# A gated DeltaNet stage on one core: convolution taps that read PSUM, an inverse that goes block by block, and small scalings on other engines

## The chip, the cores and the metric

The kernel runs on one core of a Trainium2 chip (trn2). The metric is the device time of one execution in microseconds. In the profile TensorE is PE (its weight loads PEld), VectorE is DVE, ScalarE is ACT, GpSimd is POOL, and SyncE, which issues the loads of the weights, is SP.

## The reference

Two transformer blocks run over one sequence of 256 tokens and 1024 features. The change touches one branch of the second block, a DeltaNet of 8 heads of 128 features, once forward and once backward over the sequence:

```python
def gated_deltanet_branch(qkv, z, b_in, a_in, conv_w, a_log, dt_bias, o_gain):
    qkv = jax.nn.silu(centred_depthwise_conv(qkv, conv_w))     # 5 taps, zeros at both ends
    q, k, v = jnp.split(qkv, 3, axis=-1)
    q, k, v = l2_norm(heads(q)), l2_norm(heads(k)), heads(v)
    ...
    o_fwd = chunk_gated_delta_rule(q, k, v, g[0], beta[0])
    o_bwd = flip(chunk_gated_delta_rule(flip(q), flip(k), flip(v), flip(g[1]), flip(beta[1])))
    o = rms_norm_2(o, o_gain) * jax.nn.silu(zf)

def chunk_gated_delta_rule(q, k, v, g, beta):
    ...
    lower = jnp.where(strict, jnp.einsum('bhnik,bhnjk->bhnij', k_beta, kc) * decay, 0.0)
    t_inv = lax.linalg.triangular_solve(eye + lower, eye, left_side=True, lower=True, unit_diagonal=True)
    u = t_inv @ v_beta
    w = t_inv @ (k_beta * jnp.exp(gc)[..., None])
    ...
```

The reference takes chunks of 64 tokens; the kernel computes the same function with chunks of 128, so that each head has two chunks and each chunk needs the inverse of a triangular 128x128 matrix.

## The kernel before

**Stages.** The first block runs up to about 833 us of the span and is the same in both kernels. The second block has a front stage (`block2_front`, line 1457), which computes the DeltaNet and the projections of an attention with compressed keys; then that attention, an output projection, and 16 experts, whose weights (201 MB) stream through `in_w_ex` loads of 2 MB. Those loads need the memory of the front stage's pools, so the first of them is issued when that stage ends.

**Blocks and groups.** The projection `w_qkv` has 24 blocks: q, k and v of 8 heads. A block is 24 TensorE matmuls into one PSUM bank: 8 pieces of the contracted features, each in three products of rounded parts and remainders (`mm3`, lines 169 to 171). The rounded part of a piece of weights is made by ScalarE (line 144), the remainder by VectorE (line 146). `head_in` (line 936) takes a finished block `ps`. It copies it on ScalarE into a tile `cz` with two zero columns at each end, which GpSimd sets (lines 943 to 945), scales it by the middle tap on ScalarE (line 947), and adds the four other taps on VectorE (line 949), each one 128x256 operation that reads `cz` and `cv` and writes `cv`. Then come a tanh (line 977) and the silu's product (line 978), two transposes on TensorE into another bank `pt` (line 958), and norms. The projection's `ps` and the transposes' `pt` come from the same pool of PSUM banks, tag "A", which has two.

**The chain of a group.** Two heads are a group; its chain is the generator `group` (line 1008): decays (line 1001), the matrices X (lines 1032 to 1037), and for 8 matrices at once (two directions, two chunks, two heads) the inverse Z of I + X with its transpose W (in the trace: X is AT, W is Y, Z is YT). Blocks of 16 on the diagonal are inverted column by column on VectorE (lines 1061, 1062). Then three levels join blocks of 16, 32 and 64:

```python
for m in range(8): matmul(ps[:, m], x[:, m], wv[:, m])      # line 1079, 128x128 by 64 columns
n1 = ps * mask of the level                                 # line 1081, VectorE, 128x512
for m in range(8): matmul(p2[:, m], z[:, m], n1[:, m])      # line 1094
wv = wv - p2                                                # line 1095, VectorE
8 transposes of W into PSUM, 2 copies into Z                # lines 1100, 1101 (ScalarE)
```

Level 64 needs no transposes: its second products go to half of the columns of Z or of W (lines 1087, 1089) and VectorE subtracts them (lines 1090, 1091). After the levels come the states and outputs of the two chunks (lines 1110 to 1162), with small per-token factors in a tile `small` (lines 1111 to 1116), a sum of squares `qs` (line 1024), and products with columns (`vs` line 1129, `vn1` line 1130, `q1` line 1149), all on VectorE.

**Order.** `block2_front` runs six slots. In a slot the steps of one group's projection, of the first part of the chain of the group before and of the rest of the chain of the one before that are traced in turns (`zip_longest`, line 1540). The framework then gives each engine one fixed order of instructions, made from the trace's priorities and its own planning of when operands and banks are ready. An engine whose next instruction must wait holds all that stand behind it.

Of the kernel before, what the change touches and what calls it, by code (L numbers as in the profile page):

```python
# [86 lines left out]
class B:  # L87
    """Shared helpers: streams of weight pieces, projections, norms."""
# [14 lines left out]
    def phase(self, ctx, banks, psum=None):  # L103
        """pools of one part of the kernel; banks: PSUM banks per tag; psum: what those close with, if not ctx."""
# [27 lines left out]
    def stream(self, name, group=1, pool=0):  # L132
        """Pieces of a weight, in order, each as (rounded part, remainder); pool: GpSimd subtracts one in so many."""
# [15 lines left out]
    def staged(self, n, first, second, fills):  # L149
        """second(i, first(i)) for each i, one first ahead; fills: spare blocks at the start, then per i."""  # L150
# [1599 lines left out]
```

## Time and profile before

| what | value |
|---|---|
| runs | 1752.5, 1753.26, 1753.8 us; median 1753.26 |
| profiled execution, span | 1749.7 us |
| around the span, to the median | 3.6 us |
| PE busy over the span | 1531.4 us (88%) |
| DVE busy | 919.8 us (53%) |
| ACT busy | 659.8 us (38%) |
| POOL busy | 115.5 us (7%) |

The profiled execution is shown by its span alone, from its first to its last instruction; what the device time has beside it is the third row. The busy shares are averages over stages with different limits. A row of the windows' view gives, for a stretch of the span, each engine's busy time, the TensorE clock that was granted as a share of full speed, and the share of time in which the DMA engines moved data. A row by shape gives the busy time of a group of instructions, the mean duration of one in ns, and the idle time of the engine just before them with what ended it. In a timeline an instruction's start is given in us from the span's start; matmuls overlap, so that their pace is the distance of their starts.

### The profile page before, as it was taken

How to read it: one execution, taken by the hardware profiler on the slowest of the kernel's cores; microseconds unless marked ns; L12 is line 12 of the kernel's file. 1: busy time of each engine (PE TensorE's matmuls, PEld its weight loads, DVE VectorE, ACT ScalarE, POOL GpSimd, SP SyncE). 2: the span in 40 equal slices, each digit the busy share in tenths (PEclk: the TensorE clock that was granted, in tenths of full speed). 3: DMA queues.
4: the chain of work that ended last, by engine and by line, in shares of the span. 5: the costliest groups of instructions: out<-in, count | busy, mean ns of one | idle time of the engine just before them, and what ended most of it. 6: DMA issues, size and time to landing. Idle time of an engine off the chain costs nothing. (4 is left out here: it accounts for less than half of the span.)

```text
span 1749.7 us, 25276 instructions
## 1 busy us (share of the span) xinstructions
PE 1531.4 (88%) x9987; PEld 1192.8 (68%) x9987; DVE 919.8 (53%) x1685; ACT 659.8 (38%) x1181; POOL 115.5 (7%) x196
## 2 busy tenths in 40 slices
PE   7999999999999999999879999999989856656565
PEld 7989889998887888999768878867764301211112
DVE  7665677656566567755898986545651200101001
ACT  7444554445554544444754433455321100000000
POOL 0000000000000000000251431100000000000000
PEclk9999999999999999999889999999989988878878
DMA  6655489655545348865413122356769999999997
GB/s 238 184 182 164 148 282 315 219 186 175 167 136 168 121 168 300 294 193 178 138 49 98 60 85 85 134 194 246 267 233 372 427 428 427 427 428 426 428 428 313
DMA packets 76887, 416.08 MB, mean 238 GB/s; under 512 B 9696, under 2 KB 10976, under 8 KB 64480
## 3 DMA queue, kind: packets, MB, share of 16 engines
q1 hardware_dynamic: 76768, 414.47, 64.4%
q8 instruction: 78, 1.28, 0.3%
q14 instruction: 41, 0.34, 0.1%
HBM read 413.38 MB, written 1.05 MB: 237 GB/s over the span
## 5 line engine op out<-in xcount | busy, mean ns | idle before, releaser
L146 DVE TENSOR_TENSOR wl<-st,wh 128x1024 fp32r<-128x1024 f32 x350 | 429.0, 1228 | 241.2 <-PE ps L171 99.1
L144 ACT CAST wh<-st 128x1024 fp32r<-128x1024 f32 x350 | 366.6, 1049 | 426.4 <-PE ps L170 124.9
L171 PE MATMUL ps<-ah,wl 128*128 128x256 f32 x1152 | 324.0, 282 | 5.1 <-DVE wl L146 4.8
L169 PE MATMUL ps<-ah,wh 128*128 128x256 f32 x1152 | 323.7, 281 | 0.2
L170 PE MATMUL ps<-al,wh 128*128 128x256 f32 x1152 | 322.5, 280 | 0.0
L171 PEld LDWEIGHTS ps<-ah,wl 128*128 128x128 f32 x1152 | 216.8, 188 | 8.5 <-DVE wl L146 8.2
L169 PEld LDWEIGHTS ps<-ah,wh 128*128 128x128 f32 x1152 | 216.8, 188 | 2.8 <-ACT wh L144 0.6
L170 PEld LDWEIGHTS ps<-al,wh 128*128 128x128 f32 x1152 | 216.2, 188 | 2.0
L1340 PE MATMUL ps<-ex,slot 128*32 128x512 f32 x512 | 86.9, 812 | 63.1 <-DMA ex<-in_w_ex 63.1
L1298 DVE TENSOR_TENSOR room<-room,ps 128x512 f32<-128x512 f32 x8 | 5.5, 687 | 221.0 <-PE ps L1340 221.0
L169 PE MATMUL ps<-wh,ah 128*128 128x512 f32 x288 | 115.3, 400 | 0.0
L170 PE MATMUL ps<-wl,ah 128*128 128x512 f32 x288 | 114.4, 397 | 0.0
L171 PE MATMUL ps<-wh,al 128*128 128x512 f32 x288 | 114.1, 397 | 0.0
L1340 PE MATMUL ps<-ex,room 128*32 128x256 f32 (+1 forms) x768 | 74.7, 536 | 37.1 <-DMA ex<-in_w_ex 36.8
L1340 PE MATMUL ps<-ex,xe 128*32 128x512 f32 x512 | 77.2, 689 | 32.8 <-DMA ex<-in_w_ex 32.6
L1297 ACT ACTIVATE room<-ps 128x512 f32<-128x512 f32 x8 | 4.7, 596 | 268.1 <-PE ps L1340 268.0
L1340 PEld LDWEIGHTS ps<-ex,slot 128*32 128x32 f32 x512 | 16.0, 130 | 131.4 <-DMA ex<-in_w_ex 101.6
L1340 PEld LDWEIGHTS ps<-ex,room 128*32 128x32 f32 x768 | 26.2, 123 | 82.8 <-DMA ex<-in_w_ex 36.6
L808 DVE SCALAR_TENSOR_TENSOR sm<-sm,csil 128x1024 f32<-128x1024 f32 x48 | 58.6, 1223 | 25.3 <-DMA sm<-in_w_mod 25.1
L169 PE MATMUL ps<-wh,yh 128*128 128x512 f32 x176 | 69.6, 395 | 0.4 <-ACT yh L183 0.4
L170 PE MATMUL ps<-wl,yh 128*128 128x512 f32 x176 | 69.5, 395 | 0.0
L171 PE MATMUL ps<-wh,yl 128*128 128x512 f32 x176 | 69.4, 394 | 0.0
(494 smaller groups left out, 2608.3 us busy)
## 6 DMA issues: line engine op xcount, KB each, us to landing
ex<-in_w_ex SPq DMA_DIRECT2D x94, 2048.0 KB, 39.1
st<-in_w_ff SPq DMA_DIRECT2D x132, 512.0 KB, 4.1
sm<-in_w_mod SPq DMA_DIRECT2D x48, 512.0 KB, 5.1
st<-in_w_ci SPq DMA_DIRECT2D x24, 512.0 KB, 3.6
st<-in_w_qkv SPq DMA_DIRECT2D x24, 512.0 KB, 3.3
st<-in_w_mk SPq DMA_DIRECT2D x16, 512.0 KB, 3.6
st<-in_w_mv SPq DMA_DIRECT2D x16, 512.0 KB, 3.5
st<-in_w_mq SPq DMA_DIRECT2D x16, 512.0 KB, 3.6
```

The source lines that it names most:

```text
L144: nc.scalar.copy(hi[:, :w], st[:, q, :w])
L146: e.tensor_tensor(lo[:, :w], st[:, q, :w], hi[:, :w].bitcast(F32), ALU.subtract)
L169: mm(ps, lh[0], rh[0], start=start, stop=False)
L170: mm(ps, lh[0], rh[1], start=False, stop=False)
L171: mm(ps, lh[1], rh[0], start=False, stop=stop)
L808: nc.vector.scalar_tensor_tensor(st, st, 1.0, self.sc, ALU.mult, ALU.mult, accum_out=m[:, k:k + 1])
L1297: nc.scalar.activation(hid[:, s], gu[0][f], AF.Silu)
L1298: nc.vector.tensor_tensor(hid[:, s], hid[:, s], gu[1][f], ALU.mult)
L1340: b.nc.tensor.matmul(ps[32 * j:32 * j + 32], lhs[:, 32 * j:32 * j + 32], w[:, j], start=k == 0, stop=k == KC - 1)
```

## The change

Three parts of the DeltaNet are written anew; all else is the same.

1. **Taps.** The tile `cz`, its two GpSimd memsets and ScalarE's copy are gone. The four taps read the PSUM bank `ps` itself, over 254 or 255 columns, so that no zeros are needed. The bank is now released by the last tap.
2. **Levels 32 and 64.** Level 16 stays. Level 32 multiplies only blocks that can be other than zero: 16 products of 32x32, two copies of 32x256 (ScalarE and VectorE), 24 products of 32x32 that give the blocks of Z and of W directly, and four multiplications by -1 (three on ScalarE, one on VectorE). The mask, 8 transposes and two copies are gone. Level 64 has 8 products of 64x64, a ScalarE copy, 8 products, and a multiplication by -1 on each of VectorE and ScalarE instead of two subtractions.
3. **Small scalings.** `small` has three rows instead of four: one memset on GpSimd and two copies on ScalarE, for two memsets and three copies on VectorE. `qs` goes to GpSimd. `vn1` becomes two ScalarE scalings of 128x128 and a copy of 128x256, `q1` four ScalarE scalings of 128x128, each in place of one VectorE product of 128x512.

```diff
-LEVELS = (16, 32, 64)
...
-    lv = []
-    for b_ in LEVELS:
-        c = r[r // b_ % 2 == 0][None, :]
-        lv.append(f((k // (2 * b_) == c // (2 * b_)) & (k // b_ % 2 == 1)))
-    a['m_lev'] = np.concatenate(lv, axis=1)
+    c = r[r // SUB % 2 == 0][None, :]
+    a['m_lev'] = f((k // (2 * SUB) == c // (2 * SUB)) & (k // SUB % 2 == 1))
...
-        self.sub, self.lev = (c('m_sub', 8 + SUB), c('m_lev', len(LEVELS) * 64))
+        self.sub, self.lev = (c('m_sub', 8 + SUB), c('m_lev', 64))
...
-        z = b.sp.tile([P, T + 4], F32, tag='cz', name=b.nm('cz'))
-        nc.gpsimd.memset(z[:, 0:2], 0.0)
-        nc.gpsimd.memset(z[:, T + 2:], 0.0)
-        nc.scalar.copy(z[:, 2:T + 2], ps)
...
-            nc.vector.scalar_tensor_tensor(v, z[:, t:t + T], w(t), v, ALU.mult, ALU.add)
+            to, of = (slice(2 - t, T), slice(0, T + t - 2)) if t < 2 else (slice(0, T + 2 - t), slice(t - 2, T))
+            nc.vector.scalar_tensor_tensor(v[:, to], ps[:, of], w(t), v[:, to], ALU.mult, ALU.add)
...
-        nc.vector.tensor_scalar(self.qs[:, :, hs], self.qs[:, :, hs], EPS * P, EPS * EPS * P, ALU.mult, ALU.add)
+        nc.gpsimd.tensor_scalar(self.qs[:, :, hs], self.qs[:, :, hs], EPS * P, EPS * EPS * P, ALU.mult, ALU.add)
...
-        for li, bs in enumerate(LEVELS):
-            yield True
-            wv = W.rearrange('p d t h (n s c) -> p (d t h) n s c', s=2, c=bs)[:, :, :, 0]
-            n1 = b.dp.tile([P, 8, 64], F32, tag='n1', name=b.nm('n1'), bufs=2)
-            ps = b.psum(tag).rearrange('p (m c) -> p m c', m=8)
-            for m in range(8):
-                nc.tensor.matmul(ps[:, m].rearrange('p (n c) -> p n c', c=bs), x[:, m], wv[:, m], start=True, stop=True)
-            nc.vector.tensor_tensor(n1, ps, mid(self.lev[:, li * 64:li * 64 + 64], 8), ALU.mult)
-            p2 = b.psum(tag).rearrange('p (m c) -> p m c', m=8)
-            if bs == 64:
-                for m in range(8):
-                    if m < 4:
-                        nc.tensor.matmul(p2[0:64, m], n1[:, m], z[:, m, 64:], start=True, stop=True)
-                    else:
-                        nc.tensor.matmul(p2[64:, m], z[:, m, 64:], n1[:, m], start=True, stop=True)
-                nc.vector.tensor_tensor(z[0:64, 0:4, 64:], z[0:64, 0:4, 64:], p2[0:64, 0:4], ALU.subtract)
-                nc.vector.tensor_tensor(w[64:, 4:8, 0:64], w[64:, 4:8, 0:64], p2[64:, 4:8], ALU.subtract)
-                break
-            for m in range(8):
-                nc.tensor.matmul(p2[:, m], z[:, m], n1[:, m], start=True, stop=True)
-            nc.vector.tensor_tensor(wv, wv, p2.rearrange('p m (n c) -> p m n c', c=bs), ALU.subtract)
-            for d in range(2):
-                s = slice(4 * d, 4 * d + 4)
-                p3 = b.psum(tag).rearrange('p (h i) -> p h i', h=4)
-                for m in range(4):
-                    nc.tensor.transpose(p3[:, m], w[:, 4 * d + m], b.eye)
-                nc.scalar.copy(z[:, s], p3)
+        yield True
+        bs = SUB
+        wv = W.rearrange('p d t h (n s c) -> p (d t h) n s c', s=2, c=bs)[:, :, :, 0]
+        n1 = b.dp.tile([P, 8, 64], F32, tag='n1', name=b.nm('n1'), bufs=2)
+        ps = b.psum(tag).rearrange('p (m c) -> p m c', m=8)
+        for m in range(8):
+            nc.tensor.matmul(ps[:, m].rearrange('p (n c) -> p n c', c=bs), x[:, m], wv[:, m], start=True, stop=True)
+        nc.vector.tensor_tensor(n1, ps, mid(self.lev, 8), ALU.mult)
+        p2 = b.psum(tag).rearrange('p (m c) -> p m c', m=8)
+        for m in range(8):
+            nc.tensor.matmul(p2[:, m], z[:, m], n1[:, m], start=True, stop=True)
+        nc.vector.tensor_tensor(wv, wv, p2.rearrange('p m (n c) -> p m n c', c=bs), ALU.subtract)
+        for d in range(2):
+            s = slice(4 * d, 4 * d + 4)
+            p3 = b.psum(tag).rearrange('p (h i) -> p h i', h=4)
+            for m in range(4):
+                nc.tensor.transpose(p3[:, m], w[:, 4 * d + m], b.eye)
+            nc.scalar.copy(z[:, s], p3)
+        yield True
+        n1 = b.dp.tile([P, 8, 64], F32, tag='n1', name=b.nm('n1'), bufs=2)[:, :, 0:32]
+        q = [slice(32 * i, 32 * i + 32) for i in range(4)]
+        ps = b.psum(tag)[:, 0:T].rearrange('p (m c) -> p m c', m=8)
+        for m in range(8):
+            for i in (0, 2):
+                nc.tensor.matmul(ps[q[i + 1], m], x[q[i], m, q[i + 1]], w[q[i], m, q[i]], start=True, stop=True)
+        nc.scalar.copy(n1[q[1]], ps[q[1]])
+        nc.vector.tensor_copy(n1[q[3]], ps[q[3]])
+        p2 = b.psum(tag)[:, 0:T].rearrange('p (m c) -> p m c', m=8)
+        for m in range(8):
+            nc.tensor.matmul(p2[q[1], m], z[q[1], m, q[1]], n1[q[1], m], start=True, stop=True)
+            nc.tensor.matmul(p2[q[2], m], n1[q[3], m], z[q[3], m, q[3]], start=True, stop=True)
+            if m < 4:
+                nc.tensor.matmul(p2[q[0], m], n1[q[1], m], z[q[1], m, q[1]], start=True, stop=True)
+            else:
+                nc.tensor.matmul(p2[q[3], m], z[q[3], m, q[3]], n1[q[3], m], start=True, stop=True)
+        nc.scalar.mul(w[q[1], :, q[0]], p2[q[1]], -1.0)
+        nc.vector.tensor_scalar(z[q[2], :, q[3]], p2[q[2]], -1.0, None, ALU.mult)
+        nc.scalar.mul(z[q[0], 0:4, q[1]], p2[q[0], 0:4], -1.0)
+        nc.scalar.mul(w[q[3], 4:8, q[2]], p2[q[3], 4:8], -1.0)
+        yield True
+        n1 = b.dp.tile([P, 8, 64], F32, tag='n1', name=b.nm('n1'), bufs=2)
+        ps = b.psum(tag).rearrange('p (m c) -> p m c', m=8)
+        for m in range(8):
+            nc.tensor.matmul(ps[64:, m], x[0:64, m, 64:], w[0:64, m, 0:64], start=True, stop=True)
+        nc.scalar.copy(n1[64:], ps[64:])
+        p2 = b.psum(tag).rearrange('p (m c) -> p m c', m=8)
+        for m in range(8):
+            if m < 4:
+                nc.tensor.matmul(p2[0:64, m], n1[64:, m], z[64:, m, 64:], start=True, stop=True)
+            else:
+                nc.tensor.matmul(p2[64:, m], z[64:, m, 64:], n1[64:, m], start=True, stop=True)
+        nc.vector.tensor_scalar(z[0:64, 0:4, 64:], p2[0:64, 0:4], -1.0, None, ALU.mult)
+        nc.scalar.mul(w[64:, 4:8, 0:64], p2[64:, 4:8], -1.0)
...
-        small = b.sp.tile([P, 4, 2, 2], F32, tag='small', name=b.nm('small'))
-        be0, be1, es, neg_eg = [small[:, i] for i in range(4)]
-        for n, be in enumerate((be0, be1)):
-            nc.vector.memset(be[:, 1], 1.0)
-            nc.vector.tensor_copy(be[:, 0], beta[:, n, 0])
+        small = b.sp.tile([P, 3, 2, 2], F32, tag='small', name=b.nm('small'))
+        be1, es, neg_eg = [small[:, i] for i in range(3)]
+        nc.gpsimd.memset(be1[:, 1], 1.0)
+        nc.scalar.copy(be1[:, 0], beta[:, 1, 0])
...
-        nc.vector.tensor_copy(es[:, 1], self.es[:, 1, hs])
+        nc.scalar.copy(es[:, 1], self.es[:, 1, hs])
...
-        nc.vector.tensor_tensor(vn1, ps, col(be0), ALU.mult)
+        for h in range(2):
+            nc.scalar.mul(vn1[:, 0, h], ps[:, 0, h], beta[:, 0, 0, h:h + 1])
+        nc.scalar.copy(vn1[:, 1], ps[:, 1])
...
-        nc.vector.tensor_tensor(q1, ps, col(self.eg[:, :, hs]), ALU.mult)
+        for d, h in dh:
+            nc.scalar.mul(q1[:, d, h], ps[:, d, h], self.eg[:, d, h0 + h:h0 + h + 1])
```

In the changed kernel the taps are line 943, the transposes of a block line 952, level 32 lines 1093 to 1108, level 64 lines 1114 to 1123.

**TensorE, in the first group's projection, before.** `ps_1487_8900` is the fourth block's bank, `ps_1464_8775` the bank of the first block's transposes.

```order
L958 MATMUL ps_1464_8775<-c_eye_67,qkT_1454_8728 128x128 x2
L169 MATMUL ps_1487_8900<-ak_1424_8523,wh_1486_8897 128x256
L170 MATMUL ps_1487_8900<-ak_1424_8523,wh_1486_8897 128x256
L171 MATMUL ps_1487_8900<-ak_1424_8523,wl_1485_8896 128x256
L169 MATMUL ps_1487_8900<-ak_1424_8523,wh_1486_8897 128x256
```

**The same place now.** `ps_1476_8839` is the third block's bank, `ps_1463_8771` that of the first block's transposes.

```order
L171 MATMUL ps_1476_8839<-ak_1424_8523,wl_1474_8835 128x256
L169 MATMUL ps_1476_8839<-ak_1424_8523,wh_1475_8836 128x256
L170 MATMUL ps_1476_8839<-ak_1424_8523,wh_1475_8836 128x256
L952 MATMUL ps_1463_8771<-c_eye_67,qkT_1454_8728 128x128 x2
L171 MATMUL ps_1476_8839<-ak_1424_8523,wl_1474_8835 128x256
L169 MATMUL ps_1476_8839<-ak_1424_8523,wh_1475_8836 128x256
L170 MATMUL ps_1476_8839<-ak_1424_8523,wh_1475_8836 128x256
```

The transposes of a block stood behind the whole projection of the block two further on; they now stand inside it, behind 8 of its 24 matmuls here and behind 14 one block later. They take the bank that held the block between the two, which the taps of that block release.

**VectorE, where level 32 of the first group meets the taps of a block, before.** `n1`, `Y` and the `ps` beside them belong to the level, `t16` and `z16` to the blocks of 16 of the next group.

```order
L1081 TENSOR_TENSOR n1_1664_9754<-ps_1665_9755,m_lev_8688 128x512
L949 SCALAR_TENSOR_TENSOR cv_1660_9739<-cz_1659_9735,cols2_2228,cv_1660_9739 128x256
L1061 TENSOR_TENSOR t16_1670_9792<-ps_1669_9787,z16_1654_9698 128x8x15
L949 SCALAR_TENSOR_TENSOR cv_1660_9739<-cz_1659_9735,cols2_2228,cv_1660_9739 128x256
L1062 TENSOR_TENSOR z16_1654_9698<-z16_1654_9698,t16_1670_9792 128x8x15
L1095 TENSOR_TENSOR Y_1513_9053<-Y_1513_9053,ps_1666_9765 128x16x32
L978 SCALAR_TENSOR_TENSOR vraw_1661_9745<-th_1662_9746,cv_1660_9739 128x256
```

**The same place now.**

```order
L943 SCALAR_TENSOR_TENSOR cv_1645_9679<-ps_1644_9654,cols2_2228,cv_1645_9679 128x254
L1055 TENSOR_TENSOR t16_1653_9748<-ps_1652_9743,z16_1640_9642 128x8x15
L943 SCALAR_TENSOR_TENSOR cv_1645_9679<-ps_1644_9654,cols2_2228,cv_1645_9679 128x255
L1056 TENSOR_TENSOR z16_1640_9642<-z16_1640_9642,t16_1653_9748 128x8x15
L943 SCALAR_TENSOR_TENSOR cv_1645_9679<-ps_1644_9654,cols2_2228,cv_1645_9679 128x255
L1106 TENSOR_SCALAR YT_1508_9030<-ps_1651_9714 32x8x32
L943 SCALAR_TENSOR_TENSOR cv_1645_9679<-ps_1644_9654,cols2_2228,cv_1645_9679 128x254
L1055 TENSOR_TENSOR t16_1654_9751<-ps_1652_9743,z16_1640_9642 128x8x14
```

Between the taps of a block stand operations of the next group's chain, as before. The level's mask and its subtraction over 128 rows are no longer there; a multiplication over 32 rows stands between the third and fourth tap, and the taps read `ps_1644_9654`.

## Rows read from the trace of the kernel before

**Rows 1.** The page, part 1: busy time and instructions.

```profile
PE 1531.4 (88%) x9987; PEld 1192.8 (68%) x9987; DVE 919.8 (53%) x1685; ACT 659.8 (38%) x1181; POOL 115.5 (7%) x196
```

**Rows 2.** Windows: us; PE, PEld, DVE, ACT, POOL; clock; DMA, GB/s.

```profile
857.00:937.00 80.00, 63.83 (x441) 58.91 (x440) 75.08 (x186) 42.38 (x112) 34.95 (x60) 0.89 0.27 88
937.00:1022.00 85.00, 78.51 (x650) 74.14 (x650) 75.19 (x192) 38.29 (x109) 25.35 (x44) 1.00 0.21 69
1022.00:1135.00 113.00, 106.02 (x711) 92.67 (x710) 73.89 (x156) 45.16 (x88) 25.42 (x29) 0.98 0.31 103
...
1312.00:1749.00 437.00, 286.30 (x2042) 90.64 (x2041) 41.09 (x93) 23.57 (x47) 3.10 (x5) 0.84 0.97 411
```

**Rows 3.** Line 1697's loads: ns min/median/max, first and last start.

```profile
L1697 SPq DMA_DIRECT2D ex<-in_w_ex x98: 327/328/1109, 1129.3 to 1704.0; - x98
```

**Rows 4.** DVE by shape, 857 to 937: busy us, mean ns, idle before.

```profile
L949 DVE SCALAR_TENSOR_TENSOR cv<-cz,cols,cv 128x256 f32<-128x256 f32 x53 | 33.2, 635 | 0.6 <-ACT cv L947 0.6
```

**Rows 5.** DVE by shape, 937 to 1022.

```profile
L949 DVE SCALAR_TENSOR_TENSOR cv<-cz,cols,cv 128x256 f32<-128x256 f32 x43 | 23.3, 543 | 1.3 <-ACT cv L947 1.2
...
L1081 DVE TENSOR_TENSOR n<-ps,m_lev 128x512 f32<-128x512 f32 x6 | 4.1, 683 | 0.5 <-PE ps L1079 0.5
...
L1130 DVE TENSOR_TENSOR vn<-ps,small 128x512 f32<-128x512 f32 x2 | 1.4, 683 | 0.0
...
L1090 DVE TENSOR_TENSOR YT<-YT,ps 64x256 f32<-64x256 f32 x2 | 0.8, 412 | 0.6 <-PE ps L1089 0.6
```

**Rows 6.** DVE by shape, 833 to 1090.

```profile
L1114 DVE COPY small<-es 128x2 f32<-128x2 f32 x4 | 3.1, 780 | 0.0
...
L1024 DVE TENSOR_SCALAR qs<-qs 128x4 f32<-128x4 f32 x4 | 2.6, 656 | 0.0
```

**Rows 7.** Line 949 alone: ns min/median/max, first and last start.

```profile
L949 DVE SCALAR_TENSOR_TENSOR cv<-cz,cols,cv x96: 466/478/1346, 859.9 to 1019.1; 128x256 f32<-128x256 f32 x96
```

**Rows 8.** Line 190 alone, the same columns.

```profile
L190 DVE SCALAR_TENSOR_TENSOR al<-ps,cols,ah x56: 473/475/485, 12.5 to 645.3; 128x256 fp32r<-128x256 f32 x56
```

**Rows 9.** GpSimd's timeline: start, duration, instruction.

```profile
910.49 2.48 POOL L1001 TENSOR_TENSOR dr<-rge,gr 128x512 fp32r<-128x512 f32 x2 [1.94 <-PE ps L1002]
```

**Rows 10.** DVE's timeline in the same stretch.

```profile
910.81 1.26 DVE L949 SCALAR_TENSOR_TENSOR cv<-cz,cols,cv 128x256 f32<-128x256 f32 x1
912.00 0.24 DVE L1061 TENSOR_TENSOR t<-ps,z 128x96 f32<-128x96 f32 x1
```

**Rows 11.** Timeline of three engines around one block.

```profile
1014.72 0.28 PE L171 MATMUL ps<-ak,wl 128*128 128x256 f32 x1
...
1016.14 0.48 ACT L947 ACTIVATE cv<-ps,cols 128x256 f32<-128x256 f32 x1
...
1016.72 0.48 DVE L949 SCALAR_TENSOR_TENSOR cv<-cz,cols,cv 128x256 f32<-128x256 f32 x1 [0.64 <-ACT cv L947]
...
1017.25 0.48 DVE L949 SCALAR_TENSOR_TENSOR cv<-cz,cols,cv 128x256 f32<-128x256 f32 x1
...
1019.09 0.48 DVE L949 SCALAR_TENSOR_TENSOR cv<-cz,cols,cv 128x256 f32<-128x256 f32 x1
```

**Rows 12.** PE by shape, 857 to 1022.

```profile
L958 PE MATMUL ps<-c_eye,qkT 128*128 128x128 f32 x32 | 6.7, 292 | 6.4 <-DVE qkT L978 5.8 <-DVE dg L876 0.4 <-DVE dg L878 0.2
```

**Rows 13.** PE's timeline, 950 to 962.

```profile
951.59 0.71 PE L1100 MATMUL ps<-c_eye,Y 128*128 128x128 f32 x5
...
953.20 1.89 PE L1079 MATMUL ps<-Y,AT 128*128 128x64 f32 x16
...
957.30 0.28 PE L171 MATMUL ps<-ak,wl 128*128 128x256 f32 x1
957.42 0.28 PE L169 MATMUL ps<-ak,wh 128*128 128x256 f32 x1
957.63 0.50 PE L1087 MATMUL ps<-YT,n 128*64 128x64 f32 x5
...
958.52 0.39 PE L170 MATMUL ps<-ak,wh 128*128 128x256 f32 x1
```

More of the change, by code (lines that the diff above doesn't have):

```diff
@@ L894, in __init__ @@
         self.le = c("m_le")
-        self.sub, self.lev = c("m_sub", 8 + SUB), c("m_lev", len(LEVELS) * 64)
+        self.sub, self.lev = c("m_sub", 8 + SUB), c("m_lev", 64)
         self.pick = b.xp.tile([P, SUB - 1, P], F32, tag="pick", name="pick")
@@ L1072, in group @@
             nc.scalar.copy(w[:, s], ps)
-        for li, bs in enumerate(LEVELS):
-            yield True
-            wv = W.rearrange("p d t h (n s c) -> p (d t h) n s c", s=2, c=bs)[:, :, :, 0]
-            n1 = b.dp.tile([P, 8, 64], F32, tag="n1", name=b.nm("n1"), bufs=2)
-            ps = b.psum(tag).rearrange("p (m c) -> p m c", m=8)
-            for m in range(8):
-                nc.tensor.matmul(ps[:, m].rearrange("p (n c) -> p n c", c=bs), x[:, m], wv[:, m],
-                                 start=True, stop=True)
-            nc.vector.tensor_tensor(n1, ps, mid(self.lev[:, li * 64:li * 64 + 64], 8), ALU.mult)
-            p2 = b.psum(tag).rearrange("p (m c) -> p m c", m=8)
-            if bs == 64:
-                for m in range(8):
-                    if m < 4:
-                        nc.tensor.matmul(p2[0:64, m], n1[:, m], z[:, m, 64:], start=True, stop=True)
-                    else:
-                        nc.tensor.matmul(p2[64:, m], z[:, m, 64:], n1[:, m], start=True, stop=True)
-                nc.vector.tensor_tensor(z[0:64, 0:4, 64:], z[0:64, 0:4, 64:], p2[0:64, 0:4], ALU.subtract)
-                nc.vector.tensor_tensor(w[64:, 4:8, 0:64], w[64:, 4:8, 0:64], p2[64:, 4:8], ALU.subtract)
-                break
-            for m in range(8):
-                nc.tensor.matmul(p2[:, m], z[:, m], n1[:, m], start=True, stop=True)
-            nc.vector.tensor_tensor(wv, wv, p2.rearrange("p m (n c) -> p m n c", c=bs), ALU.subtract)
-            for d in range(2):
-                s = slice(4 * d, 4 * d + 4)
-                p3 = b.psum(tag).rearrange("p (h i) -> p h i", h=4)
-                for m in range(4):
-                    nc.tensor.transpose(p3[:, m], w[:, 4 * d + m], b.eye)
-                nc.scalar.copy(z[:, s], p3)
@@ new lines, in group @@
+        yield True
+        bs = SUB
+        wv = W.rearrange("p d t h (n s c) -> p (d t h) n s c", s=2, c=bs)[:, :, :, 0]
+        n1 = b.dp.tile([P, 8, 64], F32, tag="n1", name=b.nm("n1"), bufs=2)
+        ps = b.psum(tag).rearrange("p (m c) -> p m c", m=8)
+        for m in range(8):
+            nc.tensor.matmul(ps[:, m].rearrange("p (n c) -> p n c", c=bs), x[:, m], wv[:, m], start=True, stop=True)
+        nc.vector.tensor_tensor(n1, ps, mid(self.lev, 8), ALU.mult)
+        p2 = b.psum(tag).rearrange("p (m c) -> p m c", m=8)
@@ new lines, in group @@
+        n1 = b.dp.tile([P, 8, 64], F32, tag="n1", name=b.nm("n1"), bufs=2)[:, :, 0:32]
+        q = [slice(32 * i, 32 * i + 32) for i in range(4)]
+        ps = b.psum(tag)[:, 0:T].rearrange("p (m c) -> p m c", m=8)
+        for m in range(8):
[3 more added lines that the diff above has]
+        nc.vector.tensor_copy(n1[q[3]], ps[q[3]])
+        p2 = b.psum(tag)[:, 0:T].rearrange("p (m c) -> p m c", m=8)
@@ L1102, in group @@
+        p2 = b.psum(tag).rearrange("p (m c) -> p m c", m=8)
+        for m in range(8):
[5 more added lines that the diff above has]
+        nc.scalar.mul(w[64:, 4:8, 0:64], p2[64:, 4:8], -1.0)
         yield True
@@ L1105, in group @@
         col = lambda a: a.rearrange("p d (h o) -> p d h o", o=1).to_broadcast([P, 2, 2, P])
-        small = b.sp.tile([P, 4, 2, 2], F32, tag="small", name=b.nm("small"))
-        be0, be1, es, neg_eg = [small[:, i] for i in range(4)]
-        for n, be in enumerate((be0, be1)):
-            nc.vector.memset(be[:, 1], 1.0)
-            nc.vector.tensor_copy(be[:, 0], beta[:, n, 0])
+        small = b.sp.tile([P, 3, 2, 2], F32, tag="small", name=b.nm("small"))
+        be1, es, neg_eg = [small[:, i] for i in range(3)]
+        nc.gpsimd.memset(be1[:, 1], 1.0)
+        nc.scalar.copy(be1[:, 0], beta[:, 1, 0])
         nc.vector.tensor_tensor(es[:, 0], self.es[:, 0, hs], beta[:, 0, 0], ALU.mult)
-        nc.vector.tensor_copy(es[:, 1], self.es[:, 1, hs])
+        nc.scalar.copy(es[:, 1], self.es[:, 1, hs])
         nc.vector.tensor_scalar(neg_eg, self.eg[:, :, hs], -1.0, None, ALU.mult)
```

10 lines of the change are left out of this document (6 added, 4 removed).

## Prediction

> **What bounds the kernel now.** I read the page's busy shares first: PE 88%, DVE 53% [rows 1]. Such shares mix stages, so I cut the span by stage [rows 2]. The last 437 us are bound by DMA (share 0.97), at 411 GB/s. Their loads begin only at 1129.3 [rows 3], when the front stage's pools are given back; so a microsecond won or lost before about 1130 moves everything behind it by as much, and one behind it is worth nothing. The changed lines run in three stretches, 857 to 937, 937 to 1022 and 1022 to 1135. In the first DVE is busy 75.08 of 80 us (94%) and PE 63.83 (80%): DVE is the bound. In the second PE has 78.51 and DVE 75.19 of 85 us: both are near it. In the third PE has 106.02 of 113 us, and DVE 65%: PE is the bound.
>
> Next I asked what DVE does in the first two. The taps come first: 53 take 33.2 us, then 43 take 23.3 us, with means of 635 and 543 ns [rows 4, 5], though half of all 96 take 478 ns or less and the longest 1346 [rows 7]. The timelines side by side show why: while GpSimd multiplies two SBUF tiles, from 910.49 on [rows 9], a tap that starts at 910.81 takes 1.26 us, and the operation behind it, whose first operand is in PSUM, takes its plain 0.24 us [rows 10]. A DVE operation with both inputs in SBUF is stretched beside GpSimd's work; one with an input in PSUM is not. Line 190, of the same operation and shape with one input in PSUM, shows the price that a changed tap should have: 473 to 485 ns over 56 instructions [rows 8].
>
> **The change part by part.**
>
> *Taps, DVE's work.* 96 taps at 475 ns are 45.6 us; now they take 33.2 + 23.3 = 56.5. DVE saves 10.9 us in 857 to 1022.
>
> The Trainium skill speaks against this: "Perfetto Trace Analysis", section "Optimizing Scalar/DVE Operations", gives a VectorE instruction some 60 ns of access overhead on SBUF and 125 ns on PSUM. An estimate by the Trainium skill is 96 x 65 ns = 6.2 us given back, and 1747 us instead of the sum below. The trace disagrees: 475 ns with PSUM against 478 without [rows 7, 8].
>
> *Levels and scalings, DVE's work.* Per group go: two mask products at 683 ns, one subtraction of the same width (I take 683 too), two of 64x256 at 412, and `vn1` and `q1` at 683 each: 4.24 us [rows 5]. The two small operations of lines 1114 and 1024 took 780 and 656 ns each, 1.4 us together [rows 6]. Added are three operations of at most 64x256, priced by line 1090's 412 ns (bounds: 240 ns of the small row in [rows 10] and 683): 1.2 us. Net 4.4 us per group; two of the four groups pass here before 1022, so 8.9 us. DVE's work in 857 to 1022 falls from 150.3 to 150.3 - 10.9 - 8.9 = 130.5 us.
>
> *Levels, PE's work.* Products of this stage come as two records each. Level 32 now: 16 records 1.89 us, twice, and 8 transposes at 0.71 for five, 1.1 us: 4.9 us. Level 64 now: 1.89 and 16 records of 64 columns; five of these take 0.50 us, 0.056 from start to start, so 0.9: 2.8 us [rows 13]. In the changed kernel level 32 has 80 records and level 64 has 32. At 0.056 that is 4.5 and 1.8 us. A change of the matmuls' shape costs a little: 957.42 to 957.63 is 0.21 us where projections follow each other at 0.12 [rows 13], so 0.1; three new stretches with two sides each are 0.6. Saved: 4.9 - 4.5 + 2.8 - 1.8 - 0.6 = 0.8 us per group. The bounds are half the 64-column pace, since 32 columns are half as many (+4), and the projections' pace of 0.12 for each record (-6). I take 0.056, the row nearest in size.
>
> *ACT.* It loses 24 copies and gains some ten operations per group. It is busy 42.38 of 80 and 38.29 of 85 us, half the time, so this hides; cover gone, it would show as a late scaling of the middle tap. `q1` is longer on ACT: at most four times 0.48 us [rows 11] instead of 0.68. I charge 0.5 us once, at the end of the last group's chain.
>
> *POOL.* It loses 48 memsets that waited in its queue for DVE's taps to free `cz`, and gains four small scalings. It is busy 34.95 of 80 us; nothing, as long as PE seldom waits for it.
>
> *The held bank.* This is the wait that the change adds. `ps` was free when ACT had read it; now the last tap frees it. Behind that wait on PE stand the transposes of the block before and, in PE's fixed order, the rest of the next projection. The order in "The change" shows them after 8 to 14 of that projection's matmuls instead of after 24. So the loop of a block runs in series: hold H from the projection's end to the last tap's end; two transposes, 0.4 us (292 ns each, overlapping [rows 12]); the 14 matmuls behind them at 0.12, 1.7 us [rows 13]; and whatever other PE work doesn't fall into the hold. Other PE work is 63.83 + 78.51 = 142.3 less 24 blocks of 2.9 + 0.4, which leaves 63 us or 2.6 per block; I choose a third of it outside, 0.9.
>
> H now, from one block: the last matmul starts at 1014.72 and lasts 0.28, the last tap ends at 1019.57: 4.6 us. Taps that follow each other at once are 0.53 us apart, and ACT's scaling takes 0.48 [rows 11]. So H is at least 0.48 + 4 x 0.53 = 2.6, 2.7 with the hand-overs; and at most about 4.3, today's less the copy. I choose 3.2: one short DVE operation between each two taps, as DVE's order has it, and no stretched taps. A block then takes 3.2 + 0.4 + 1.7 + 0.9 = 6.2 us. Now 24 blocks take 160 us, the taps running from 859.9 to 1019.1 [rows 7]: 6.67 each. The gain is 24 x 0.47 = 11.2 us. DVE's 130.5 us are 5.4 per block, so DVE ceases to be the bound; the loop through PSUM is late next.
>
> *Third stretch.* PE's chain gives two groups at 0.8 us, less the 0.5 of `q1`: 1 us.
>
> **Sum.** 11.2 + 1 = 12 us. The profiled span is 1749.7 and would be 1737.7; the median lies 3.6 above that span, so 1753.26 - 12 = **1741 us**.
>
> **Rivals.**
>
> *A, faster: the banks don't bind.* With H at 2.7 the loop takes 5.7 us, 137 for 24 blocks, less than PE's own work of 142.3 - 1.6 = 140.7. PE becomes the bound, and with 2 us of idle time 857 to 1022 shrinks from 165 to 143: -22, with the third stretch **1730 us**. For it: DVE's idle time before taps is small now, 0.6 and 1.3 us [rows 4, 5], so finished blocks wait for DVE, and DVE gets 20 us lighter. Against it: chain operations still stand between the taps.
>
> *B, no change: the gain is swallowed.* With H at 3.7 a block takes 6.7 us, as now: about **1753 us**. For it: PE is already at 92% in the second stretch, and operations with two SBUF inputs (lines 146, 978, 1062) remain for GpSimd to stretch, so the stretching moves instead of going. A tap dearer from PSUM would act here too.
>
> *C, slower: the held bank becomes the bound.* With H near today's, 4.3, a block takes 7.3 us: 24 x 0.63 = 15 us lost, less 1: **1767 us**. It decides from H = 3.7. For it: PE waits 5.8 us for DVE at these very transposes already [rows 12], with a bank that is released early. Against it: H of today includes DVE's queue, 94% full.
>
> *D, slower: the small products are dear.* At 0.12 us a record the levels cost 6 us more per group instead of 0.8 less; with 24 + 3 us against the forecast, **1768 us**. The 64-column row speaks against it.
>
> **How the numbers follow.** Forecast 0.46, A 0.20, B 0.17, C 0.13, D 0.04. A measurement of this kernel tells 0.2%, 3.5 us, from no change. B splits into 0.06 faster, 0.07 the same and 0.04 slower. Faster is then 0.72, the same 0.07, slower 0.21. The range goes from 1725 (A with a little less PE work) to 1766, which takes in B and the half of C with H under 4.3; what is left out is the rest of C, D and 0.04 below.
>
> **What would show it.** Right: the taps' mean near 475 ns with no long ones beside GpSimd's products; DVE's share of 857 to 937 falling under 90% with idle time before taps, waiting for ACT's scaling; PE's waits at the transposes (line 952) now on a tap (line 943), some 1 us each; 24 blocks in about 149 us; level 32 on PE near 4.5 us; the experts' first load near 1117. Wrong: taps over 540 ns; a bank held over 3.7 us from a projection's end; 32x32 records further apart than 0.1 us; or PE waiting for ACT's new operations, which I cost at nothing.

## The result, and the profile after

| | before | changed |
|---|---|---|
| median, us | 1753.53 | 1727.32 |
| runs, us | 1752.5 to 1757.62 | 1724.7 to 1732.84 |
| profiled execution: device time, span | | 1725.69, 1724.0 |

The ratio of the times is 0.9866, with a 95% interval of 0.9845 to 0.9886: 23.5 us faster, between 20 and 27. I had forecast 12.

The page of the changed kernel, part 1, answers to [rows 1]:

```profile
PE 1512.3 (88%) x10147; PEld 1169.0 (68%) x10147; DVE 892.6 (52%) x1645; ACT 667.1 (39%) x1209; POOL 117.0 (7%) x156
```

TensorE lost 19 us of busy time and VectorE 27. To see where the span became shorter I cut the front stage at three marks: from the first tap to the first product of level 16 (A), from there to the start of the last tap (B), and from there to the first load of the experts' weights (C). The marks of before are in [rows 3, 7] and in this row of line 1079, whose last columns are the first and the last start:

```profile
L1079 PE MATMUL ps<-Y,AT x192: 217/275/323, 936.7 to 1110.0; 128*128 128x64 f32 x192
```

Those of the changed kernel, from the views of its lines 943, 1074 and 1721:

```profile
L943 DVE SCALAR_TENSOR_TENSOR cv<-ps,cols,cv x96: 376/475/485, 857.2 to 1002.4; 128x254 f32<-128x254 f32 x48, 128x255 f32<-128x255 f32 x48
```
```profile
L1074 PE MATMUL ps<-Y,AT x64: 217/275/322, 927.5 to 1070.3; 128*128 128x64 f32 x64
```
```profile
L1721 SPq DMA_DIRECT2D ex<-in_w_ex x98: 327/328/652, 1105.9 to 1678.9; - x98
```

A went from 76.8 to 70.3 us, B from 82.4 to 74.9, C from 110.2 to 103.5; the stage from 269.4 to 248.7, so 20.7 shorter. The other 5 us of the two spans' difference lie in code that is the same in both, 2.7 before the first tap and 2.3 behind the first load; a second execution of the changed kernel started its taps 4.7 us later and had the same 70.3, 74.9 and 103.5. These three parts are therefore the finer measure, though each kernel's are read from one execution, and the device time is the judge.

The windows of A, B and C before (columns as in [rows 2]):

```profile
859.90:936.70 76.80, 60.63 (x413) 55.71 (x412) 71.88 (x174) 40.18 (x107) 34.13 (x58) 0.89 0.26 84
936.70:1019.10 82.40, 76.88 (x643) 73.04 (x642) 72.59 (x185) 37.77 (x106) 24.03 (x42) 1.00 0.22 72
1019.10:1129.30 110.20, 102.75 (x696) 89.96 (x694) 74.45 (x156) 42.97 (x80) 25.82 (x29) 0.98 0.27 87
```

And in the changed kernel:

```profile
857.20:927.50 70.30, 56.24 (x397) 51.29 (x397) 61.46 (x172) 36.51 (x100) 33.49 (x34) 0.95 0.26 85
927.50:1002.40 74.90, 71.50 (x723) 66.71 (x722) 61.95 (x163) 40.53 (x113) 22.87 (x26) 0.98 0.25 79
1002.40:1105.90 103.50, 96.56 (x789) 82.50 (x787) 68.08 (x144) 51.50 (x109) 29.08 (x31) 1.00 0.30 98
```

In A VectorE is 10.4 us lighter and no longer 94% busy but 87%; it is still the busiest engine there, since TensorE has 80%. In C TensorE is 6.2 us lighter, and C is 6.7 us shorter, though I had given it 1 us. Summed over the three windows TensorE is busy 224.3 us where it was 240.3: of the 20.7 us, 16.0 are less busy time of TensorE and 4.7 less idle time. TensorE's timeline at levels 32 and 64 of the first group shows where its work went (the two groups in C have the same pace):

```profile
935.92 0.69 PE L1093 MATMUL ps<-Y,AT 32*32 32x32 f32 x32
...
939.58 0.21 PE L1099 MATMUL ps<-n,YT 32*32 32x32 f32 x1
939.58 0.21 PE L1100 MATMUL ps<-YT,n 32*32 32x32 f32 x1
939.59 0.21 PE L1102 MATMUL ps<-YT,n 32*32 32x32 f32 x1
...
940.08 0.19 PE L1100 MATMUL ps<-YT,n 32*32 32x32 f32 x1
...
943.23 1.14 PE L1114 MATMUL ps<-Y,AT 64*64 64x64 f32 x16
```

Three records start within 0.01 us, each of them 0.2 us long. The first 32 records start (0.69 - 0.19) / 31 = 0.016 us apart, the other 48, from 939.58 to 940.08, 0.011. Level 32 takes 1.3 us of TensorE where I had 4.5.

Last, the view of line 943 tells who waited for a tap, and TensorE's waits from 855 to 1110 (in us in total, times, longest) tell what it did wait for:

```profile
who waited for it (us, times):
  ACT th L971: 8.9, 8
  PE ps L169: 0.2, 1
```
```profile
PE ps L952 <- DVE vraw L972: 5.4, 3, 2.7
PE ps L1065 <- POOL YT L1062: 3.1, 4, 1.5
PE ps L952 <- DVE qkT L972: 2.8, 4, 1.1
```

One wait of 0.2 us is all that TensorE's waits owe to the held bank. The transposes (line 952) wait for the silu, as before [rows 12], and not for a tap. It isn't that the hold is short. From the end of a projection's last matmul to the end of its block's last tap it lasts 5.2 us on average over the 24 blocks, from 2.6 to 8.4 (before, by the same reading, 7.6). One block, from its last matmul to its last tap, with the last matmul of the next block between them:

```profile
894.66 0.28 PE L171 MATMUL ps<-ak,wl 128*128 128x256 f32 x1
...
901.71 0.28 PE L171 MATMUL ps<-ak,wl 128*128 128x256 f32 x1
...
902.25 0.47 DVE L943 SCALAR_TENSOR_TENSOR cv<-ps,cols,cv 128x254 f32<-128x254 f32 x1
```

This bank is held from 894.94 to 902.72, 7.8 us, and the whole next projection runs meanwhile, into the other bank.

**A correction.** The text ahead of the prediction says that a block's projection and its transposes take their banks from the same pool, "A", and that the transposes take a bank which taps release. That is wrong. `steps_ws` has M as its own default, so the projections use the two banks of M and only the transposes use A. Transposes can't wait for a bank that taps hold; only the projection two blocks on can.

### The profile page after: what moved, and what is told of

The parts are those of the page before. It is cut to its first block, busy times and chain, and to the rows that moved or that the text cites. A ratio compares the mean times of both kernels' runs of the same rounds, so it can differ in the third digit from the quotient of the medians.

```text
span 1724.0 us, 25507 instructions
## 1 busy us (share of the span) xinstructions
PE 1512.3 (88%) x10147; PEld 1169.0 (68%) x10147; DVE 892.6 (52%) x1645; ACT 667.1 (39%) x1209; POOL 117.0 (7%) x156
## 4 chain that ended last, share of the span: by engine, by line
PE 59%; DMA 25%; DVE 8%; POOL 3%; issue 3%; ACT 2%; SPq 0%; DVEq 0%; POOLq 0%; ACTq 0%
DMA ex<-in_w_ex 20%; PE ps L169 15%; PE ps L171 15%; PE ps L170 15%; PE ps L1364 3%; DVE wl L146 2%; DMA sm<-in_w_mod 2%; PE ps L480 1%; DMA st<-in_w_ff 1%; PE ps L250 1%; PE ps L1471 1%; PE ps L501 1%; DVE cv L943 1%; POOL dr L995 1%; PE ps L1050 1%
## 5 line engine op out<-in xcount | busy, mean ns | idle before, releaser
L1364 PE MATMUL ps<-ex,xe 128*32 128x512 f32 x512 | 78.6, 700 | 34.1 <-DMA ex<-in_w_ex 33.9
L1364 PEld LDWEIGHTS ps<-ex,xe 128*32 128x32 f32 x512 | 15.4, 119 | 80.4 <-DMA ex<-in_w_ex 52.5
```

The lines of the kernel that those rows point to most:

```text
L1364: b.nc.tensor.matmul(ps[32 * j:32 * j + 32], lhs[:, 32 * j:32 * j + 32], w[:, j], start=k == 0, stop=k == KC - 1)
```

## The experiments

### The three parts, alone and in pairs

Each part was undone or kept as it stands in the diff ahead: `taps_only`, `levels_only` and `small_only` keep one part, `no_taps`, `no_small` and `taps_small` two. The edits are those three groups of lines, so that `no_small` for example is

```diff
-        for d, h in dh:
-            nc.scalar.mul(q1[:, d, h], ps[:, d, h], self.eg[:, d, h0 + h:h0 + h + 1])
+        nc.vector.tensor_tensor(q1, ps, col(self.eg[:, :, hs]), ALU.mult)
...
```

with `vn1`, `small` and `qs` taken back likewise. Expected of one part alone:

> The kernel before with the first part alone: the taps read PSUM, no copy, no memsets. Theory 1 (the blocks' stretch was bound by VectorE, and the taps were what GpSimd stretched; the held bank costs nothing): taps near 475 ns, the 24 blocks shortened by 6 to 10 us, the third stretch unchanged, 6 to 10 us faster in all. Theory 2 (TensorE's work sets the time nearly everywhere, and the gain is that of the products of levels 32 and 64): under 4 us faster. Theory 3 (the held bank does cost, hidden in the sum): no faster or slower.

> The kernel before with the second part alone: levels 32 and 64 block by block, without masks and transpositions. Theory 1: TensorE does some 4 us less per group; two groups fall in the third stretch, where TensorE is the bound, 6 to 8 us there, and at most 4 us more before it, since VectorE stays the bound there: 7 to 12 us faster. Theory 2: 15 us or more, all four groups count.

> The kernel before with the third part alone: the small scalings on ScalarE and GpSimd. Theory 1: VectorE loses some 3 us per group, of which the two groups before the third stretch can count: 2 to 5 us faster. Theory 2: nothing, within 2 us.

Of two parts, and of the changed kernel run once more:

> The changed kernel with the first part undone: copy, memsets and taps from SBUF as before, levels and scalings as in the change. Theory 1: the blocks' stretch is again bound by VectorE with stretched taps; 6 to 10 us slower than the changed kernel, so 13 to 18 us faster than before. Theory 2: within 4 us of the changed kernel. Theory 3: faster than the changed kernel.

> The changed kernel with the third part undone: taps from PSUM and the new levels, small scalings on VectorE as before. Taps alone gave 1 us and levels alone 13. Joint theory (VectorE and TensorE are both close to full, relief of one shows only when the other is relieved too): the two together give 18 to 23 us, more than the sum of their single gains, and the third part adds 0 to 4. Additive rival: 13 to 15 us, and the third part makes up the rest.

> The changed kernel with the second part undone: taps and scalings as in the change, levels as before, so VectorE is lighter by both and TensorE has all its old products. Joint theory: TensorE holds the stage, 0 to 4 us faster than before though VectorE loses some 15 us of work. Rival (VectorE was the bound): 8 us or more.

> The changed kernel itself, unedited, beside the variants of this series. Theory: 1.2 to 1.5% faster than before, and the front stage, from the first tap to the first load of the experts' weights, about 20 us shorter.

Measured (ratio to the kernel before, in its interval; A, B, C and the stage from the same three marks, in us):

| kernel | parts | ratio | interval | A | B | C | stage |
|---|---|---|---|---|---|---|---|
| before | none | 1 | | 76.8 | 82.4 | 110.2 | 269.4 |
| taps_only | 1 | 0.9993 | 0.9979 to 1.0007 | 69.3 | 94.1 | 107.2 | 270.6 |
| levels_only | 2 | 0.9925 | 0.9898 to 0.9953 | 77.9 | 78.6 | 105.7 | 262.2 |
| small_only | 3 | 0.9995 | 0.9976 to 1.0014 | 75.9 | 87.4 | 105.7 | 269.0 |
| taps_small | 1, 3 | 0.9978 | 0.9963 to 0.9993 | 71.6 | 92.9 | 106.9 | 271.4 |
| no_taps | 2, 3 | 0.9891 | 0.9871 to 0.9912 | 77.6 | 76.3 | 99.1 | 253.0 |
| no_small | 1, 2 | 0.9875 | 0.9854 to 0.9896 | 69.1 | 82.4 | 102.2 | 253.7 |
| after_again | 1, 2, 3 | 0.9862 | 0.9839 to 0.9884 | 70.3 | 74.9 | 103.5 | 248.7 |

The parts alone shorten the stage by -1.2, 7.2 and 0.4 us, 6.4 together; all three shorten it by 20.7. Relief of one engine shows where the other is relieved too: the joint theory holds, the additive one falls, and so does theory 1 for the taps alone, which was to give 6 to 10 us. The device times agree, with less room: alone 0.07, 0.75 and 0.05%, together 0.87 (give or take 0.36), against 1.34 and 1.38 for the three; and the two parts of `no_small` give 22 us (18 to 26), where the additive rival had 13 to 15. The stage of `levels_only` may be on the long side: its times run from 1731.3 to 1743.85 us, and the execution shown took 1740.39. For the levels alone theories 1 and 2 aren't told apart, since 13 us was measured with an interval from 8 to 18. Its row of the whole stage shows what the levels lack alone:

```profile
856.40:1118.60 262.20, 230.00 (x1899) 203.87 (x1897) 211.92 (x502) 127.56 (x308) 87.89 (x128) 0.95 0.24 83
```

TensorE is busy 10.3 us less than before and idle 3.1 us more. The levels are the part without which nothing is gained in the stage (`taps_small`: 2.0 us longer, and by its ratio at most 0.4% faster). The taps' undoing, which I expected to cost 6 to 10 us, costs 4.3 (253.0 against 248.7). Beside them the taps give 8.5 us (262.2 to 253.7), the scalings 9.2 (262.2 to 253.0), and both 13.5.

**Where the taps' own gain went.** A is 7.5 us shorter with the taps alone, as I had it, and B 11.7 us longer. The windows of A, B and C of `taps_only`:

```profile
860.10:929.40 69.30, 55.66 (x400) 50.86 (x400) 61.80 (x175) 36.36 (x96) 33.06 (x32) 0.97 0.25 86
929.40:1023.50 94.10, 87.32 (x667) 82.68 (x666) 73.38 (x191) 36.08 (x93) 23.33 (x27) 0.91 0.22 74
1023.50:1130.70 107.20, 100.70 (x683) 88.65 (x681) 70.20 (x148) 43.14 (x80) 23.17 (x26) 0.98 0.24 84
```

In B the granted clock is 0.91 where it was 1.00. It isn't an accident of one execution: the windows of B of `taps_small` and of `no_small`, which have the taps too, show 0.93 and 0.92.

```profile
932.00:1024.90 92.90, 85.77 (x667) 81.36 (x666) 68.83 (x179) 39.42 (x109) 25.50 (x30) 0.93 0.22 75
929.20:1011.60 82.40, 77.18 (x731) 71.86 (x731) 64.97 (x172) 38.54 (x101) 22.12 (x24) 0.92 0.23 78
```

Narrower windows of `taps_only` at the beginning of B show the fall, and the timeline what TensorE did ahead of it:

```profile
920.00:924.00 4.00, 4.00 (x29) 3.58 (x29) 4.00 (x17) 2.35 (x5) 0.00 (x0) 1.00 0.32 105
924.00:928.00 4.00, 2.18 (x17) 1.69 (x15) 3.89 (x18) 2.46 (x7) 1.59 (x2) 1.00 0.06 26
928.00:932.00 4.00, 3.64 (x19) 3.46 (x17) 1.40 (x5) 1.17 (x2) 2.52 (x3) 0.57 0.00 0
932.00:936.00 4.00, 3.22 (x16) 3.03 (x15) 2.39 (x4) 0.42 (x1) 0.00 (x0) 0.50 0.01 4
936.00:940.00 4.00, 3.68 (x17) 3.39 (x17) 2.48 (x4) 0.31 (x3) 0.00 (x0) 0.50 0.00 0
940.00:944.00 4.00, 4.00 (x28) 4.00 (x27) 3.19 (x7) 1.55 (x6) 1.60 (x1) 0.72 0.51 162
```
```profile
927.52 0.66 PE L1069 MATMUL ps<-c_eye,YT 128*128 128x128 f32 x4 [1.52 <-POOL YT L1066]
928.54 1.11 PE L1069 MATMUL ps<-c_eye,YT 128*128 128x128 f32 x4 [0.36 <-POOL YT L1066]
```

TensorE was busy 2.18 of 4 us and waited 1.52 and 0.36 us for GpSimd's block-diagonal products; then the clock stood at its lower level (0.50, 1.2 of 2.4 GHz) from some time after 928 to some time after 940, while TensorE had work for 80% of it or more. The waits alone don't explain that. The changed kernel has the same two, and its clock falls later and comes back sooner:

```profile
925.99 0.66 PE L1065 MATMUL ps<-c_eye,YT 128*128 128x128 f32 x4 [1.53 <-POOL YT L1062]
927.00 0.66 PE L1065 MATMUL ps<-c_eye,YT 128*128 128x128 f32 x4 [0.36 <-POOL YT L1062]
```
```profile
928.00:932.00 4.00, 3.22 (x29) 3.08 (x29) 2.40 (x4) 0.38 (x2) 0.97 (x1) 1.00 0.01 4
932.00:936.00 4.00, 3.69 (x22) 3.27 (x23) 3.43 (x6) 1.81 (x8) 0.10 (x1) 0.57 0.00 0
936.00:940.00 4.00, 4.00 (x96) 3.82 (x99) 3.18 (x9) 1.05 (x3) 1.50 (x1) 1.00 0.78 244
```

Why it stayed low longer in `taps_only` is open.

B has 94.1 x 0.09 = 8.5 us less of full clock than before, of the 11.7 us that it is longer. Such a count is an upper bound. In A, where TensorE isn't the busiest, a better clock went with next to no gain: `small_only` has 0.96 there for 0.89, 5.4 us of full clock more, and A is 0.9 us shorter.

```profile
857.00:932.90 75.90, 57.34 (x411) 52.05 (x410) 70.92 (x168) 40.42 (x111) 37.28 (x60) 0.96 0.25 84
```

B of `taps_only` also has 667 records of TensorE for 643, and A and C have 13 fewer each: part of the shift between the three is work that moved across a mark. By the same count (length times one minus clock) the whole stage lost 10.6 us before, 12.7 in `taps_only`, 8.7 in `no_small`, and 5.0 with all three parts. So part of what the parts give in company, at most 5.6 of the 20.7 us, is TensorE's clock.

### The pace of the small products

```diff
-        for m in range(8):
-            for i in (0, 2):
+        for i in (0, 2):
+            for m in range(8):
...
```

and likewise one loop for each kind of the 24 products behind it.

> The changed kernel with the same 40 products of 32x32 per group at level 32 in another order: eight of one place in the array behind each other, instead of two or three places in turns. All other work is the same. If products in different places of the array run at once, and TensorE's work counts one for one: 32 and 48 records take 0.06 us each instead of 0.02 and 0.013, some 3.5 us more per group, 8 to 14 us slower than the change. If the pace is a matter of the small size alone, or TensorE's work doesn't count: the same within 3 us.

Ratio to before 0.9902 (0.9873 to 0.9930), against 0.9862 and 0.9866 for the change; A 70.3, B 80.0, C 105.4, stage 255.7: 7.0 us longer. TensorE's timeline at the last group:

```profile
1083.13 1.09 PE L1093 MATMUL ps<-Y,AT 32*32 32x32 f32 x32
...
1086.31 0.69 PE L1099 MATMUL ps<-n,YT 32*32 32x32 f32 x16
...
1087.58 0.59 PE L1101 MATMUL ps<-YT,n 32*32 32x32 f32 x13
...
1088.25 0.32 PE L1105 MATMUL ps<-n,YT 32*32 32x32 f32 x5
```

(1.09 - 0.19) / 31 = 0.029 us from record to record, where two places in turns had 0.016. So products in different places of the array do run at once, and one place alone takes half of the 0.056 us that records of 64 columns had [rows 13]. I had expected 0.06, so the size was off by half, and with it the 8 to 14 us. The 32 records cost 0.4 us more. The 48, from first to last start, take 0.50 and 0.80 us where they had 0.50, so 0.8 more. That is near 5 us over four groups; the stage grew by 7. The window of B shows where more can have gone:

```profile
925.50:1005.50 80.00, 76.62 (x722) 71.71 (x721) 61.86 (x162) 40.49 (x113) 22.86 (x26) 0.94 0.22 74
```

The clock is 0.94 in place of 0.98, at most some 3 us. The intervals of the two ratios overlap, so that the device time alone wouldn't show it. The Trainium skill, "TensorEngine Tiling (Array Packing)", section "Key Properties", says that different tiles of the array can load weights and multiply in parallel; 0.011 and 0.016 against 0.029 agree.

### The source of the taps

```diff
+        z = b.sp.tile([P, T], F32, tag="cz", name=b.nm("cz"))
+        nc.scalar.copy(z, ps)
...
-            nc.vector.scalar_tensor_tensor(v[:, to], ps[:, of], w(t), v[:, to], ALU.mult, ALU.add)
+            nc.vector.scalar_tensor_tensor(v[:, to], z[:, of], w(t), v[:, to], ALU.mult, ALU.add)
```

> The changed kernel with taps that read an SBUF copy of the block which ScalarE makes, without zero columns and memsets: the bank is free early, and the tap has two SBUF inputs again. Theory: taps beside GpSimd's products are stretched to about 1 us again, VectorE gets 6 to 10 us more work in the blocks' stretch, 4 to 9 us slower than the change. If the memsets in GpSimd's queue or the held bank were what mattered: the same as the change, or faster.

Ratio 0.9901 (0.9878 to 0.9923); the stage is 255.5, 6.8 us longer than with the change, A 79.1 against 70.3. The view of its line 945:

```profile
L945 DVE SCALAR_TENSOR_TENSOR cv<-cz,cols,cv x96: 462/478/1291, 860.5 to 1015.5; 128x254 f32<-128x254 f32 x48, 128x255 f32<-128x255 f32 x48
```

Without memsets, with the bank free early and the same columns, the taps again reach 1291 ns, where line 943 has at most 485. By the timelines, 18 of its 96 taps take over 600 ns, and 15 of these run beside GpSimd products of two tiles; in the change 31 taps run beside such products and none is long. Eight taps in a row take 0.85 us each here:

```profile
876.22 1.04 POOL L997 TENSOR_TENSOR dr<-rlt,gr 128x512 fp32r<-128x512 f32 x1
...
876.36 6.80 DVE L945 SCALAR_TENSOR_TENSOR cv<-cz,cols,cv 128x254 f32<-128x254 f32 x8
877.22 2.40 POOL L997 TENSOR_TENSOR dr<-rge,gr 128x512 fp32r<-128x512 f32 x2
```

For the stretching it counts that one input is in PSUM; neither the memsets nor the bank do. The 6.8 us also hold ScalarE's copy, which was not priced apart.

### The held bank

Three kernels tried the bank.

```diff
-        pt = b.psum(tag).rearrange("p (t d) -> p t d", d=P)
+        pt = b.psum("M").rearrange("p (t d) -> p t d", d=P)
```

> The changed kernel with a block's transposes in a PSUM bank of the pool M, which the taps never hold, instead of pool A, whose two banks then serve projections alone. If the held bank costs something (the loop that the prediction counted in series): 4 us or more faster than the change. If it costs nothing, as the waits of the trace say (one wait of 0.2 us for a tap): the same within 3 us.

Ratio 1.0219 (1.0202 to 1.0237), stage 312.3: 63.6 us longer than with the change. The expectation had the pools wrong, see the correction: the edit doesn't part transposes from projections, it puts both into the two banks of M. It built a loop in series, of the kind that I had costed. TensorE's order now has the transposes of each block before the next projection, 24 blocks take (1095.6 - 860.2) / 24 = 9.8 us each, and VectorE waits for TensorE (857 to 1180):

```profile
DVE wl L146 <- PE ps L171: 42.8, 17, 6.5
DVE qkT L972 <- ACT th L971: 12.2, 11, 5.1
```

The second kernel holds the bank longer. The tanh goes into the free half of the same bank:

```diff
-        self.silu2(s, v)
+        self.silu2(s, v, bank[:, T:2 * T])
...
-        th = b.sp.tile([P, T], F32, tag="th", name=b.nm("th"), bufs=1)
         nc.scalar.activation(th, v, AF.Tanh)
```

> The changed kernel with ScalarE's tanh written into the free half of the block's PSUM bank, so that the silu's product has one input in PSUM; the bank is then held for 1 us more, until that product has run. Theory: the product's mean falls from 0.54 to near 0.42 us, some 2 to 3 us less for VectorE; 0 to 3 us faster than the change. If the held bank costs: slower by 4 us or more.

Ratio 0.9948 (0.9928 to 0.9969), stage 260.8, 12.1 us longer than with the change, though the silu's product became faster, as the groups by shape show:

```profile
L972 DVE SCALAR_TENSOR_TENSOR qkT<-ps,cv 128x256 f32<-128x256 f32 x16 | 6.7, 418 | 2.3 <-ACT ps L971 2.2
```

It had 544 ns in the change, so the 24 products of this line save 3 us of VectorE. Yet the stage is 12 us longer with a bank that is held for a tanh and a product more. Among TensorE's waits there is none of a projection for the product that releases the bank. But the planner also moved TensorE's order: here nearly all transposes stand between whole projections. How much is the hold and how much the order wasn't separated.

The third gives M a bank more, at the cost of one of N1:

```diff
-            b.phase(ctx, {"A": 2, "M": 2, "N0": 2, "N1": 2})
+            b.phase(ctx, {"A": 2, "M": 3, "N0": 2, "N1": 1})
```

> The changed kernel with three PSUM banks instead of two in pool M, from which the projections take theirs, and one instead of two in N1, which the chains of the first and third group use. If the held bank still costs in the change (a bank held 1 us longer, for the silu, cost 12 us of the front stage): the stage falls from 248.7 us by 4 us or more, and the kernel is faster than the change. If two banks are enough as long as only the taps hold them: the stage stays within 3 us, or grows, since the two groups' chains have one bank less.

Ratio 0.9904 (0.9884 to 0.9923), stage 253.2, 4.5 us longer than the change; A is 70.3, the same to a tenth. In A a third bank brings nothing, unless the bank that N1 lost, where the first group's chain runs, took just as much: two banks seem enough for a hold that ends with the taps. B is 4.2 us longer; that fits N1's loss, but was not tested apart.

No kernel of the series beat the change.

## Why the prediction was right or wrong

- **The sign and the mechanism of the taps: right.** Taps at 475 ns and none over 485; `sbuf_taps` brings the stretching back, and A with it. The PSUM read isn't dearer, so that the rule of the Trainium skill weighed there ("Perfetto Trace Analysis", section "Optimizing Scalar/DVE Operations") finds no support: 475 ns at the median from PSUM, 478 from SBUF in `sbuf_taps`.
- **"The held bank", the loop of a block: wrong.** This step set 11.2 us as the gain of A and B, where 14.0 were measured. It came near by chance. The loop rests on a pool that the code doesn't share (the default argument of `steps_ws` says M); the profile after shows one wait of 0.2 us. The hold H was wrong too: I chose 3.2 us, from one block of 4.6 before, and it is 5.2 on average (7.6 before). With that the loop would take 8.2 us per block, longer than in rival C, while the 24 blocks' taps, from 857.2 to 1002.4, come 6.05 us apart: a bank's hold and the next projection overlap, they don't add up. The result is that of rival A (the banks don't bind, 1730 us), but again in part by luck: its condition was a hold of 2.7 us, it had 22 us in A and B and 1 in C, and 14.0 and 6.7 were measured.
- **"Levels, PE's work": the term that was mis-sized.** I gave 0.8 us per group. Level 32 takes 1.3 us for 4.5, since I put the pace of 64 columns on 32 (0.056), and products in several places overlap (0.011 to 0.016). Level 64 takes 1.1 and 0.9, 2.0 for 1.8. With the same 4.9 and 2.8 before and 0.6 for changes of shape that is 3.8 us per group, 15.2 for four, near the 16.0 that TensorE's busy time fell by. My upper bound of +4 held it; I had taken the row nearest in size instead of asking what smaller tiles do at the same time.
- **"Third stretch", 1 us: wrong for the same reason.** Two groups at 3.8 are 7.6; C is 6.7 shorter. `q1` on ScalarE is not seen to cost anything.
- **"VectorE ceases to be the bound": right in B (83% busy, TensorE 95%), not in A, and it pays only in company.** `taps_only` shows VectorE 10 us lighter in A, A 7.5 us shorter, and no gain over the stage. I had no term for what the relief of one engine is worth without that of the other.
- **TensorE's clock: left out.** [rows 2] had it at 0.89 in the first stretch; no term of the sum allows for a change. By the count above it is at most 5.6 us of the stage's 20.7.
- **ACT and POOL at nothing: nothing speaks against it.** ScalarE is busy 51.50 of C's 103.50 us, and neither is in TensorE's waits with more than the 3.1 us of a GpSimd product that stood there before.

## What to carry to other kernels

Where two engines are both near full, price a relief in the pairs of the edits, not one by one: alone the taps were worth nothing here, beside the levels 8.5 us. Before costing a wait for a PSUM bank, find the pool from which each tile is taken, defaults included. And where an operation with two SBUF inputs on VectorE runs beside GpSimd's work, see whether one input can stay in PSUM.

## What the runs showed of the hardware that was not expected

- Products of 32x32 in different places of the array start 0.011 to 0.016 us apart, in one place 0.029, records of 64 columns 0.056: 80 small records take less time than 16 large ones with their 1.89 us.
- After the same waits of 1.5 and 0.4 us on TensorE the clock was low for some 14 us in `taps_only` (the granted shares of its windows from 928 to 944) and for about 3 in the changed kernel, while TensorE had work for 80% of the time or more. So two variants of this stage can differ by some microseconds of clock though TensorE's waits are the same.
- `scalar_tensor_tensor` over 128x254 takes 475 ns with one input in PSUM and 478 with both in SBUF, at the median; beside GpSimd's products only the second form is stretched, up to 1291 ns. The silu's product shows the same: 544 ns from SBUF on average, 418 with its tanh in PSUM.
- The front stage of the changed kernel came out the same to 0.1 us in two executions, while its device times lay up to 8 us apart: a stage's own marks can tell what the whole time can't.
